# Two heads' values side by side in the array, and a new order at both ends of an expert product

## The chip, the cores and the metric

One core of a Trainium2 chip. A core has TensorE (PE: matmuls; its weight loads are listed as PEld), VectorE (DVE), ScalarE (ACT), GpSimd (POOL) and SyncE (SP, which here only issues transfers), and DMA engines that move data between HBM and the on-chip memory SBUF. Matmuls write into PSUM. Each engine works through its own queue in order; semaphores make one wait for another. The metric is the time of one execution in microseconds.

## The reference

Two layers of an encoder over 512 tokens of width 1024. A layer has a mixing block (8 retention heads and 8 dilated attention heads of 64, joined and projected), an attention over 256 memory rows, and an expert layer (128 x 128 = 16384 experts per layer, 8 heads x 16 chosen per token). The parts that matter here, shortened:

```python
for layer in range(DEPTH):
    rq, rk, rv, rg, aq, ak, av = jnp.split(rms_norm(x, norm_mix[layer]) @ w_in[layer], split_points, axis=-1)
    ret = bidirectional_retention(rq, rk * HEAD_DIM ** -0.5, rv, log_gamma)   # (q k^T * decay(i-j)) v, per head
    att = dilated_mixture_attention(aq, ak, av)      # three softmaxes over bands, mixed: one softmax with a bias
    cat = [head_rms_norm(ret) * silu(rg), head_rms_norm(att)]
    x = x + concatenate(cat) @ w_out[layer]
    x = x + memory_cross_attention(...)
    # experts: per token and head the 16 best of 128 x 128 pairs of keys
    act = gelu(einsum('thkd,td->thk', expert_down[idx], xb))
    x = x + einsum('thk,thkd->td', softmax(best) * act, expert_up[idx])
return rms_norm(x, norm_final)
```

## The kernel before

Tokens lie in 4 blocks of 128 (NB); a 512 x 512 score matrix of one head is 4 key blocks of 128 x 512. The program is written in the order of the work; a planner then puts each engine's instructions in an order of its own, by a simulated timeline, so that ready work of a later step (projections above all) fills PE where an earlier one waits. Tiles have a fixed number of buffers (bufs); a new tile of the same name waits until its buffer is free. Two number forms are used in matmuls: fp32r (one record of PE per matmul), in which an operand is split in a high and a low part by ACT and DVE (split, L112) and three products are made in place of one, and plain fp32 (two records per matmul, and two weight loads).

**The mixing block** (mix, L305) projects the values (L331), then runs two loops over the heads. heads (L279) projects queries and keys of four heads at a time and hands out one head after another.
- Retention (L336): DVE and ACT make a mask of decays (dm, two buffers), PE makes the scores of a key block (L345, keys down the partitions, queries along), DVE multiplies them by the mask (L348) into pt. Then L353, in fp32: for each query block qb and key block kb, pt's 128 x 128 part is the stationary operand and the head's 64 columns of values are streamed. The result has queries on the partitions; ACT copies it into cat (L355).
- Attention (L366): the same with a bias from HBM (L370, two buffers, 448 KB each), scores with queries on the partitions (L375), maximum on DVE (L379), exponential on ACT (L381), four transposes (L384), a copy by ACT or DVE (L387, L389), and the product with the values per query block (L391, as L353). DVE divides by the sums on the way into cat (L394). At head 7 (KH) the memory rows are normalised (mem_norm).

**The expert layer** treats blocks 0 to 2 (DB, 384 tokens) densely, with every expert, and block 3 by gathering its chosen rows (sparse, L567; POOL issues the gathers, DVE multiplies). The dense part goes by 128 rows i1 of 128 experts. For each: down (L667) loads the row's down weights, splits them, makes 24 products of 384 columns into one of two banks pj (L675) and a GELU on ACT (L678). 64 of the rows (KEPT, those with i % 8 > 3) have their down product made earlier (ahead, L681), while routes are still being computed, and stored in HBM (Cd); kept (L687) loads them again. up_parts (L698) loads the row's up weights into the pool late, splits them (w_hi, w_lo: 3 buffers), multiplies c by the gates (gt, L695) and splits c (ch, cl: 2 buffers). up (L709) makes 6 products of 512 columns per token block, accumulating over all rows in six banks of PSUM.

rest (L719) sets the order: per group of 8 rows the gates are loaded, then a full row and a kept row alternate, each with its up product at once. In between, steps of the gather loop are taken (take). The up products of the last two rows are held back and made block by block, each followed by the addition to x (L751), so that the next layer's norm, or the final one, can begin on block 0 early. layer (L593) opens and closes the pools: the pool late, whose tiles hold the up weights, lies where the routes' tiles lay before.

Of the kernel before, what the change touches and what calls it, by code (L numbers as in the profile page):

```python
# [8 lines left out]
F32 = mybir.dt.float32  # L9
F32R = mybir.dt.float32r  # L10
# [11 lines left out]
D = 1024  # L22
# [28 lines left out]
UR = 4  # L51
FIRST = (0, 1, 2, 3), (3, 0, 1, 2)
# [10 lines left out]
class Kernel:  # L63
# [77 lines left out]
    def wsplit(self, src, pool=None):  # L141

        raw = self.wload(src, pool)
        hi = (pool or self.wp).tile([128, D], F32R, name="w_hi", bufs=3)
        lo = (pool or self.wp).tile([128, D], F32R, name="w_lo", bufs=3)
        self.split(hi, lo, raw)
        return hi, lo
# [156 lines left out]

    def mix(self, l, kvp):  # L305
        nc, a, ps = self.nc, self.a, self.ps
        with ExitStack() as st:
# [28 lines left out]
            for h, q, ks in self.heads(ea, w, 0, 512, hT, 1.0, HD ** -0.5):  # L336
                dm = ea.tile([128, WREL], F32, name="dm", bufs=2)
                nc.vector.tensor_scalar(dm, relp, lg[:, h:h + 1], None, op0=OP.mult)
                nc.vector.scalar_tensor_tensor(dm, reln, lg[:, 8 + h:9 + h], dm, op0=OP.mult, op1=OP.add)
                nc.scalar.activation(dm, dm, AF.Exp)  # L340
                pts = []
                for kb in range(NB):
                    s = ps.tile([128, 512], F32, name="s", bufs=2)
                    for i in range(2):
                        nc.tensor.matmul(s, ks[i][:, kb * 128:(kb + 1) * 128], q, start=(i == 0), stop=(i == 1))  # L345
                    pt = ea.tile([128, 512], F32, name="pt", bufs=5)
                    o = 384 - 128 * kb
                    nc.vector.tensor_mul(pt, s, dm[:, o:o + 512])  # L348
                    pts.append(pt)
                po = ps.tile([128, NB, HD], F32, name="og"[h % 2])  # L350
# [15 lines left out]
            for h, q, ks in self.heads(ea, w, 2048, 2560, hT, HD ** -0.5, 1.0):  # L366
                if h == KH:
                    kT = self.mem_norm(l, sb)
                bias = ea.tile([128, WREL], F32, name="dm", bufs=2)
                nc.sync.dma_start(bias, a["att_bias"][h])  # L370
                po = ps.tile([128, NB, HD], F32, name="og"[h % 2])
                for qb in range(NB):
                    s = ps.tile([128, 512], F32, name="s", bufs=2)
                    for i in range(2):
                        nc.tensor.matmul(s, q[:, qb * 128:(qb + 1) * 128], ks[i], start=(i == 0), stop=(i == 1))  # L375
                    p = ea.tile([128, 512], F32, name="p", bufs=3)
                    m = ea.tile([128, 2], F32, name="m", bufs=4)
                    o = 384 - 128 * qb
                    nc.vector.tensor_tensor_reduce(p, s, bias[:, o:o + 512], 1.0, -3e38, OP.add, OP.max, m[:, 0:1])  # L379
                    nc.vector.tensor_scalar(m[:, 1:2], m[:, 0:1], -1.0, None, op0=OP.mult)  # L380
                    nc.scalar.activation(p, p, AF.Exp, bias=m[:, 1:2], accum_out=den[:, h, qb:qb + 1])  # L381
                    tp = ps.tile([128, 4, 128], F32, name="t", bufs=2)
                    for kb in range(NB):
                        nc.tensor.transpose(tp[:, kb, :], p[:, kb * 128:(kb + 1) * 128], self.ident)  # L384
# [554 lines left out]
```

## Time and profile before

| | us |
|---|---|
| median of 3 runs | 3547.29 (3547.2 to 3551.07) |
| the profiled execution | 3550.38 |
| its span, first to last instruction | 3548.6 |
| PE busy | 3473.6 (98%), 20844 records |
| DVE busy | 2645.4 (75%) |
| ACT busy | 1470.2 (41%) |
| mean granted PE clock | 0.991 of full speed |

The execution has these stretches in layer 0 (layer 1 repeats them about 1770 us later): retention about 53 to 158 us, attention to 292, output projection, memory attention and routes to about 850, a transition to 990 in which rows are gathered and the last kept rows made, and the dense part to 1771. A matmul's time in a row is its own, from start to a modelled end; matmuls overlap, so the pace of a run of them is the distance of starts. "Idle before" in square brackets is how long the engine stood before an instruction, and what ended it.

### The profile page before, as it was taken

The numbers are of one execution on the slowest core, as the hardware profiler recorded it, in microseconds if no ns is written. First come the engines' busy times: TensorE is split into PE (matmuls) and PEld (weight loads), VectorE is DVE, ScalarE is ACT, GpSimd is POOL, SyncE is SP. The second block draws the span as 40 slices with busy tenths as digits, with TensorE's granted clock in tenths as the row PEclk, the third lists the DMA queues.
The fourth block names the chain that finished last, engine by engine and source line by source line (L and its number), as shares of the span: only waits on it lengthen the run. The fifth ranks groups of instructions, "written<-read, shape, count | busy, mean of one in ns | idle before, by whom it ended". The sixth has DMA issues, their size and how long they took to land.

```text
span 3548.6 us, 55359 instructions
## 1 busy us (share of the span) xinstructions
PE 3473.6 (98%) x20844; PEld 3182.7 (90%) x20844; DVE 2645.4 (75%) x5722; ACT 1470.2 (41%) x2210; POOL 699.7 (20%) x518
## 2 busy tenths in 40 slices
PE   8999999999999999999999999999999999999998
PEld 7989998999888888888889899989999888888887
DVE  5565559998677788888555655599995877888885
ACT  4453544455333333333333535445553333333332
POOL 0000000002334445444100000000022443444440
PEclk9999999999999999999999999999999999999999
DMA  5252444567989999999432424446689999999992
GB/s 163 74 144 84 146 136 138 207 224 285 389 302 350 341 340 332 340 340 337 154 98 79 133 90 155 133 135 218 220 300 378 328 337 343 344 332 341 343 335 94
DMA packets 428380, 848.42 MB, mean 239 GB/s; under 512 B 28112, under 2 KB 278992, under 8 KB 421968
## 3 DMA queue, kind: packets, MB, share of 16 engines
q1 hardware_dynamic: 321360, 488.32, 41.2%
q0 software_dynamic: 73728, 268.47, 20.8%
q10 hardware_dynamic: 33024, 88.10, 6.9%
q8 instruction: 163, 2.67, 0.3%
q14 instruction: 105, 0.86, 0.1%
HBM read 754.60 MB, written 77.59 MB: 235 GB/s over the span
## 4 chain that ended last, share of the span: by engine, by line
PE 90%; DVE 6%; DMA 2%; ACT 1%; issue 1%; SPq 0%; ACTq 0%; POOL 0%; DVEq 0%; POOLq 0%
PE pj L675 28%; PE pj L174 13%; PE s L715 10%; PE t L715 10%; PE pj L190 9%; PE o L715 5%; PE g L715 5%; PE s L345 1%; DVE w_lo L114 1%; PE g L391 1%; PE s L375 1%; PE t L384 1%; PE g L353 1%; PE o L353 1%; PE g L873 1%
## 5 line engine op out<-in xcount | busy, mean ns | idle before, releaser
L114 DVE TENSOR_TENSOR w_lo<-w_raw,w_hi 128x1024 fp32r<-128x1024 f32 x696 | 849.4, 1222 | 404.1 <-ACT w_hi L113 391.7
L113 ACT ACTIVATE w_hi<-w_raw 128x1024 fp32r<-128x1024 f32 x696 | 735.3, 1060 | 981.6 <-PE g L715 342.8
L578 POOL DMA_INDIRECT row<-in_expert_down,ei x256 | 339.0, 1324 | 2308.3 <-PE g L874 916.8
L675 PE MATMUL pj<-hT_hi,w_hi 128*128 128x384 f32 x2048 | 697.7, 341 | 12.8 <-ACT c L678 10.5
L675 PE MATMUL pj<-hT_lo,w_hi 128*128 128x384 f32 x2048 | 698.8, 341 | 0.0
L675 PE MATMUL pj<-hT_hi,w_lo 128*128 128x384 f32 x2048 | 696.0, 340 | 0.8 <-DVE w_lo L114 0.6
L578 POOL DMA_INDIRECT row<-in_expert_up,ei x256 | 360.0, 1406 | 454.2 <-DVE x L590 419.3
L675 PEld LDWEIGHTS pj<-hT_hi,w_hi 128*128 128x128 f32 x2048 | 386.3, 189 | 18.3 <-ACT c L678 11.1
L675 PEld LDWEIGHTS pj<-hT_hi,w_lo 128*128 128x128 f32 x2048 | 386.1, 189 | 5.6 <-DVE w_lo L114 2.4
L675 PEld LDWEIGHTS pj<-hT_lo,w_hi 128*128 128x128 f32 x2048 | 386.2, 189 | 4.4
L590 DVE SCALAR_TENSOR_TENSOR x<-row,act,x 128x1024 f32<-128x1024 f32 x256 | 327.7, 1280 | 6.0 <-DMA row<-in_expert_up,ei 4.6
L584 DVE SCALAR_TENSOR_TENSOR row<-row,hn 128x1024 f32<-128x1024 f32 x256 | 309.4, 1219 | 19.9 <-DMA row<-in_expert_down,ei 19.5
L113 ACT ACTIVATE ch<-c 128x384 fp32r<-128x384 f32 x128 | 67.0, 523 | 280.2 <-PE g L715 240.1
L715 PE MATMUL t<-w_lo,ch 128*128 128x512 f32 x512 | 160.7, 389 | 0.0
L715 PE MATMUL t<-w_hi,ch 128*128 128x512 f32 x512 | 159.6, 389 | 0.0
L715 PE MATMUL s<-w_hi,ch 128*128 128x512 f32 x512 | 158.5, 391 | 0.0
L715 PE MATMUL s<-w_lo,ch 128*128 128x512 f32 x512 | 158.1, 390 | 0.0
L190 PE MATMUL pj<-w_hi,T_hi 128*128 128x256 f32 x640 | 156.9, 286 | 0.9 <-ACT T_hi L113 0.5
L715 PE MATMUL s<-w_hi,cl 128*128 128x512 f32 x512 | 157.8, 389 | 0.0
L715 PE MATMUL t<-w_hi,cl 128*128 128x512 f32 x512 | 157.7, 389 | 0.0
L113 ACT ACTIVATE ch<-cd 128x384 fp32r<-128x384 f32 x128 | 66.6, 520 | 208.9 <-PE g L715 208.9
L174 PE MATMUL pj<-T_hi,w_hi 128*128 128x512 f32 (+1 forms) x512 | 150.0, 341 | 2.1 <-DVE qlo L260 1.8
(260 smaller groups left out, 7291.9 us busy)
## 6 DMA issues: line engine op xcount, KB each, us to landing
w_raw<-in_down_T SPq DMA_DIRECT2D x256, 512.0 KB
w_raw<-in_expert_up SPq DMA_DIRECT2D x256, 512.0 KB
Gd<-mq ACTq DMA_DIRECT2D x48, 1024.0 KB
gt<-Gd SPq DMA_DIRECT2D x32, 1536.0 KB
w_raw<-in_peer_w_query SPq DMA_DIRECT2D x64, 512.0 KB
w_raw<-in_w_in SPq DMA_DIRECT2D x56, 512.0 KB
Cd<-c ACTq DMA_DIRECT2D x128, 192.0 KB
cd<-Cd SPq DMA_DIRECT2D x128, 192.0 KB
```

The costliest lines, as they stand in the source:

```text
L113: self.nc.scalar.activation(hi, src, AF.Copy)
L114: self.nc.vector.tensor_sub(lo, src, hi)
L174: nc.tensor.matmul(ps[:, :T], wt[k // 4][x][:, k % 4, s * 128:(s + 1) * 128], hT[y][:, k, :T], start=(k == 0 and x == y), stop=(k == KT - ...
L190: nc.tensor.matmul(ps[:, :256], hT[x][:, k, ts], wt[k // 4][y][:, k % 4, :], start=(k == 0 and x == y), stop=(k == KT - 1 and (x, y) == pa ...
L345: nc.tensor.matmul(s, ks[i][:, kb * 128:(kb + 1) * 128], q, start=(i == 0), stop=(i == 1))
L353: nc.tensor.matmul(po[:, qb, :], pts[kb][:, qb * 128:(qb + 1) * 128], rv[:, kb, h * HD:(h + 1) * HD], start=(kb == 0), stop=(kb == NB - 1))
L375: nc.tensor.matmul(s, q[:, qb * 128:(qb + 1) * 128], ks[i], start=(i == 0), stop=(i == 1))
L578: nc.gpsimd.indirect_dma_start(out=t, out_offset=None, in_=tab, in_offset=bass.IndirectOffsetOnAxis(ap=ei[:, j:j + 1], axis=0))
L584: nc.vector.scalar_tensor_tensor(t, t, 1.0, self.hn, op0=OP.mult, op1=OP.mult, accum_out=act[:, j:j + 1])
L590: nc.vector.scalar_tensor_tensor(x, t, act[:, j:j + 1], x, op0=OP.mult, op1=OP.add)
L675: k.nc.tensor.matmul(pa[:, :ND], x[:, kk, :], y[:, kk, :], start=(kk == 0 and x is dh and y is hi), stop=(kk == KT - 1 and x is dl))
L715: self.k.nc.tensor.matmul(self.acc[b, h], cc[x][:, s], uu[y][:, h * 512:(h + 1) * 512], start=(b, h) not in self.started, stop=last and x ...
```

## The change

In both head loops heads are taken in pairs. half_av makes the product with the values turned round: the head's 64 columns of values of a key block are the stationary operand, the score columns are streamed, and the result has the head's 64 dimensions on 64 partitions, the even head on 0 to 63, the odd on 64 to 127 of one bank. In the retention 512 columns are streamed per key block, in two groups of two key blocks x two heads; in the attention 128 per query block, 4 key blocks x 2 heads in a group. turned copies the bank to SBUF (ACT), transposes it back in four blocks, and a copy (retention, ACT) or the division (attention, DVE) puts both heads into cat. The masks or biases of both heads of a pair are made before the pair's scores. The memory rows' norm comes before heads 6 and 7 rather than 7.

In rest three down products (EARLY) are made before anything else, and each full row's up product is followed by the down product of a row three further on. The first up product is put behind the third down product on PE (issue_after). The last four rows (HELD) are held back for the blocks, with four buffers of w_hi, w_lo, ch and cl in place of 3, 3, 2 and 2, and five of c in place of 4; the gather loop's steps are spread over two rows fewer.

```diff
+HELD = 4
+EARLY = 3
...
-        hi = (pool or self.wp).tile([128, D], F32R, name="w_hi", bufs=3)
+        hi = (pool or self.wp).tile([128, D], F32R, name="w_hi", bufs=HELD if pool else 3)
...
+    def half_av(self, po, h, v, pt, kb):
+        r = slice(64 * (h % 2), 64 * (h % 2) + 64)
+        self.nc.tensor.matmul(po[r, :], v[:, h * HD:(h + 1) * HD], pt, start=(kb == 0), stop=(kb == NB - 1))
+
+    def turned(self, sb, po):
+        t = sb.tile([128, S], F32, name="oT")
+        self.nc.scalar.activation(t, po, AF.Copy)
+        tp = self.ps.tile([128, NB, 128], F32, name="t", bufs=2)
+        for qb in range(NB):
+            self.nc.tensor.transpose(tp[:, qb, :], t[:, qb * 128:(qb + 1) * 128], self.ident)
+        return tp
...
-                for qb in range(NB):
-                    for kb in range(NB):
-                        nc.tensor.matmul(po[:, qb, :], pts[kb][:, qb * 128:(qb + 1) * 128],
-                                         rv[:, kb, h * HD:(h + 1) * HD], start=(kb == 0), stop=(kb == NB - 1))
-                nc.scalar.activation(cat[:, :, h * HD:(h + 1) * HD], po, AF.Copy)
+            it = self.heads(ea, w, 0, 512, hT, 1.0, HD ** -0.5)
+            for m, two in enumerate(zip(it, it)):
...
+                po = ps.tile([128, 512], F32, name="og"[m % 2])
+                for k0 in range(0, NB, 2):
+                    pts = []
+                    for kb in range(k0, k0 + 2):
+                        for (h, q, ks), dm in zip(two, dms):
...
+                            pts.append((kb, h, pt))
+                    for kb, h, pt in pts:
+                        self.half_av(po, h, rv[:, kb], pt, kb)
+                tp = self.turned(ea, po)
+                nc.scalar.activation(cat[:, :, m * 128:(m + 1) * 128], tp, AF.Copy)
...
-                    for kb in range(NB):
-                        nc.tensor.matmul(po[:, qb, :], pt[:, kb, :], av[:, kb, h * HD:(h + 1) * HD],
-                                         start=(kb == 0), stop=(kb == NB - 1))
+                        for h, pt in pts:
+                            self.half_av(po[:, qb * 128:(qb + 1) * 128], h, av[:, kb], pt[:, kb, :], kb)
+                tp = self.turned(ea, po)
...
-        c = self.sb.tile([128, ND], F32, name="c", bufs=4)
+        c = self.sb.tile([128, ND], F32, name="c", bufs=5)
...
-        ch = self.late.tile([128, ND], F32R, name="ch", bufs=2)
+        ch = self.late.tile([128, ND], F32R, name="ch", bufs=HELD)
...
-            if n < NK - 2:
+            if n == 0:
+                with k.tc.issue_after(self.at):
+                    self.up(parts, 0, nb)
+            elif n < NK - HELD:
                 self.up(parts, 0, nb)
...
-            owed += left / (NK - 4)
+            owed += left / (NK - HELD - 2)
...
+        full = iter([i for i in range(NK) if i not in kept])
+        cs = [self.down(next(full)) for _ in range(EARLY)]
         for g in range(NK // GI):
             gt = self.gates(pool, g)
...
                 for i1 in pair:
-                    c = self.kept(kept[i1]) if i1 in kept else self.down(i1)
+                    c = self.kept(kept[i1]) if i1 in kept else cs.pop(0)
                     add(self.up_parts(c, gt[:, :, i1 % GI, :], i1))
+                    if i1 not in kept:
+                        cs += [self.down(i) for i in itertools.islice(full, 1)]
...
         for b in range(nb):
-            self.up(last[0], b, b + 1)
-            self.up(last[1], b, b + 1, True)
+            for i, parts in enumerate(last):
+                self.up(parts, b, b + 1, i == HELD - 1)
```

## Rows read from the trace of the kernel before

**Rows 1.** the page, busy time by engine, and the shares of the chain
```profile
PE 3473.6 (98%) x20844; PEld 3182.7 (90%) x20844; DVE 2645.4 (75%) x5722; ACT 1470.2 (41%) x2210; POOL 699.7 (20%) x518
PE 90%; DVE 6%; DMA 2%; ACT 1%; issue 1%; SPq 0%; ACTq 0%; POOL 0%; DVEq 0%; POOLq 0%
```

**Rows 2.** windows: stretch: length, busy us (instructions) per engine, PEclk, DMA share, GB/s
```profile
53.00:158.00 105.00, 104.57 (x697) 95.22 (x698) 60.20 (x86) 40.77 (x54) 0.00 (x0) 1.00 0.34 98
176.00:292.00 116.00, 112.46 (x711) 98.19 (x709) 72.62 (x193) 61.04 (x119) 0.00 (x0) 0.99 0.41 114
952.00:986.00 34.00, 26.79 (x127) 25.41 (x126) 22.23 (x31) 12.94 (x18) 8.68 (x7) 0.85 1.02 379
986.00:1754.00 768.00, 768.00 (x3713) 680.32 (x3712) 606.51 (x752) 275.67 (x373) 308.07 (x221) 1.00 0.92 321
```

**Rows 3.** timeline of PE in one retention head: start, us, engine, line
```profile
77.00 3.01 PE L353 MATMUL o<-rv,pt 128*128 128x64 f32 x26
79.82 0.48 PE L345 MATMUL s<-Q,K 128*128 128x512 f32 x1
```

**Rows 4.** lines of the retention stretch: busy, mean ns, idle before
```profile
L353 PE MATMUL o<-rv,pt 128*128 128x64 f32 x128 | 16.0, 268 | 0.0
```

**Rows 5.** timeline of PE: f32 products of 128 and of 256 columns
```profile
677.27 0.61 PE L539 MATMUL s<-keysT,b 128*128 128x128 f32 x4
677.71 0.22 PE L873 MATMUL g<-oh,oh 128*128 128x128 f16 x1
678.63 3.67 PE L174 MATMUL pj<-hq,w_raw 128*128 128x256 f32 x16
682.14 0.61 PE L539 MATMUL s<-keysT,b 128*128 128x128 f32 x4
```

**Rows 6.** timeline of PE: eight transposes and what follows
```profile
219.01 1.04 PE L384 MATMUL t<-ident,p 128*128 128x128 f32 x8
219.81 0.48 PE L375 MATMUL s<-K,Q 128*128 128x512 f32 x1
```

**Rows 7.** lines of the attention stretch
```profile
L391 PE MATMUL o<-rv,pt 128*128 128x64 f32 x128 | 15.9, 270 | 0.0
L387 ACT ACTIVATE pt<-t 128x512 f32<-128x512 f32 x16 | 9.5, 594 | 13.2 <-PE t L384 13.1
```

**Rows 8.** timeline of SP: a bias load in the attention
```profile
246.68 9.97 SPq L370 DMA_DIRECT2D dm<-in_att_bias  x2
```

**Rows 9.** timeline of PE at the start of the dense part, both layers
```profile
956.68 0.69 PE L675 MATMUL pj<-hT_hi,w_hi 128*128 128x384 f32 x1 [4.22 <-ACT c L678]
961.88 0.35 PE L675 MATMUL pj<-hT_hi,w_hi 128*128 128x384 f32 x1
2723.40 0.69 PE L675 MATMUL pj<-hT_hi,w_hi 128*128 128x384 f32 x1 [6.26 <-ACT c L678]
```

**Rows 10.** the chain in order of time: start, us, what; a run of down products
```profile
920.86 23.29 PE pj L675 x134
```

**Rows 11.** timelines of ACT and SP at the same places
```profile
935.91 7.47 SPq L138 DMA_DIRECT2D w_raw<-in_expert_up  x1
955.19 1.06 ACT L113 ACTIVATE w_hi<-w_raw 128x1024 fp32r<-128x1024 f32 x1 [8.78 <-DMA cd<-Cd]
2721.91 1.06 ACT L113 ACTIVATE w_hi<-w_raw 128x1024 fp32r<-128x1024 f32 x1 [12.72 <-DMA w_raw<-in_expert_up]
```

**Rows 12.** timeline at the change of layers
```profile
1771.52 0.34 SPq L75 DMA_DIRECT2D gain<-in_norm_mix  x1
1777.76 1.97 PE L123 MATMUL t<-ident,nr_h 128*128 128x128 f32 x8 [6.27 <-DVE nr_h L109]
```

**Rows 13.** timeline at the end
```profile
3535.90 0.39 PE L715 MATMUL o<-w_hi,cl 128*128 128x512 f32 x1
3536.13 0.39 PE L715 MATMUL g<-w_hi,cl 128*128 128x512 f32 x1
3543.57 1.28 DVE L109 SCALAR_TENSOR_TENSOR nr_h<-x,rs_y,gain 128x1024 f32<-128x1024 f32 x1
```

More of the change, by code (lines that the diff above doesn't have):

```diff
@@ L1 @@
+import itertools
 import math
@@ new lines, in mix @@
+                biases = []
+                for h, q, ks in two:
+                    bias = ea.tile([128, WREL], F32, name="dm", bufs=2)
+                    nc.sync.dma_start(bias, a["att_bias"][h])
+                    biases.append(bias)
+                po = ps.tile([128, 512], F32, name="og"[m % 2])
+                for qb in range(NB):
+                    pts = []
+                    for (h, q, ks), bias in zip(two, biases):
+                        s = ps.tile([128, 512], F32, name="s", bufs=2)
+                        for i in range(2):
+                            nc.tensor.matmul(s, q[:, qb * 128:(qb + 1) * 128], ks[i], start=(i == 0), stop=(i == 1))
+                        p = ea.tile([128, 512], F32, name="p", bufs=3)
+                        mx = ea.tile([128, 2], F32, name="m", bufs=4)
+                        o = 384 - 128 * qb
+                        nc.vector.tensor_tensor_reduce(p, s, bias[:, o:o + 512], 1.0, -3e38, OP.add, OP.max, mx[:, 0:1])
+                        nc.vector.tensor_scalar(mx[:, 1:2], mx[:, 0:1], -1.0, None, op0=OP.mult)
+                        nc.scalar.activation(p, p, AF.Exp, bias=mx[:, 1:2], accum_out=den[:, h, qb:qb + 1])
+                        tp = ps.tile([128, 4, 128], F32, name="t", bufs=2)
+                        for kb in range(NB):
+                            nc.tensor.transpose(tp[:, kb, :], p[:, kb * 128:(kb + 1) * 128], self.ident)
+                        pt = ea.tile([128, 4, 128], F32, name="pt", bufs=5)
+                        if h % 2:
+                            nc.scalar.activation(pt, tp, AF.Copy)
+                        else:
+                            nc.vector.tensor_copy(pt, tp)
+                        pts.append((h, pt))
+                    for kb in range(NB):
+                        for h, pt in pts:
+                            self.half_av(po[:, qb * 128:(qb + 1) * 128], h, av[:, kb], pt[:, kb, :], kb)
@@ L399, in mix @@
+                if m % 2:
+                    self.norm_heads(sb, cat, gcat, 2 + m // 2)
             early.close()
@@ L674, in down @@
             for x, y in ((dh, hi), (dh, lo), (dl, hi)):
-                k.nc.tensor.matmul(pa[:, :ND], x[:, kk, :], y[:, kk, :], start=(kk == 0 and x is dh and y is hi),
-                                   stop=(kk == KT - 1 and x is dl))
-        c = self.sb.tile([128, ND], F32, name="c", bufs=4)
+                self.at = k.nc.tensor.matmul(pa[:, :ND], x[:, kk, :], y[:, kk, :], stop=(kk == KT - 1 and x is dl),
+                                             start=(kk == 0 and x is dh and y is hi)).ins
+        c = self.sb.tile([128, ND], F32, name="c", bufs=5)
         k.nc.scalar.activation(c, pa[:, :ND], AF.Gelu_apprx_tanh)
```

67 lines of the change are left out of this document (24 added, 43 removed).

## The prediction

> **What bounds the kernel now.** I read the page first: TensorE (PE) is busy for 3473.6 of the 3548.6 us and the chain of waits lies on it for 90% [rows 1]. So only two things can pay: less PE time, or less of the 75 us in which PE stands still. Then the stretches: in the retention PE is busy for 104.6 of 105 us while DVE has 60 and ACT 41; in the attention 112.5 of 116, with DVE at 72.6 and ACT at 61; the dense part proper is PE without a gap (768 of 768), and its start loses 7.2 of 34 us [rows 2]. The change works in all three places.
>
> Then the price of what is replaced. The product of scores and values is 16 fp32 matmuls a head, and each is two records of PE (the groups count 512 for 16 heads x 16). One of them streams only 64 columns, yet 26 in a row take from 77.00 to 79.82, 0.1085 us each [rows 3]. An fp32 product of 128 columns takes the same, 4 from 677.27 to 677.71, 0.110 us; one of 256 takes 16 from 678.63 to 682.14, 0.219 us [rows 5]. So time goes with the columns above 128 and has a floor at about 0.108 us below, which 64 columns do not get under: with 128 stationary columns, half the time of each such product is wasted.
>
> **The change part by part.** *Values.* Removed: 8 heads x 16 x 2 = 256 records in the retention of a layer and as many in its attention, at 0.1085 us: 27.8 us each, 111 us in all four.
>
> Added in the retention: 4 matmuls a head, 64 records a layer, of 512 columns: twice the 256 column price, 0.438 us, 28.0 us if they run one after another. In the attention 256 records of 128 columns at 0.110 us: 28.2 us. So with one after another nothing is gained by the swap itself (28.0 and 28.2 against 27.8). All hangs on whether the two heads of a pair overlap: each has 64 stationary columns and writes one half of the partitions, and the loops alternate the heads. Nothing in this trace uses half the columns; the bounds are no overlap (0.438 and 0.110 us a record) and two at a time (half). I take the overlap, since a head's matmuls share neither output partitions nor stationary columns with the other's, and PE is the engine where a second, idle half is there. It is not quite half: the two records of one matmul follow each other on the same half, so a group of 8 records takes 5 steps and one of 16 takes 9. Retention: 8 groups x 5 x 0.438 = 17.5 us. Attention: 16 groups x 9 x 0.110 = 15.8 us. Gain 10.3 + 12.0 = 22.3 us a layer, **-44.6** in both.
>
> The result now comes out turned. Four transposes a pair, 16 pairs: eight stand from 219.01 to 219.81, 0.10 us each [rows 6], 64 of them: **+6.4**. Ahead of each stands a copy on ACT of 512 columns (0.594 us, as L387 [rows 7]), and in the retention a second one; they replace shorter ones. ACT (41 of 105, 61 of 116) has the room; PE fills their time with projection products, as it does now, and where no projection is left each costs its 0.6 us, 4 pairs at most, 2.4 us.
>
> Going from whole-array products to half-array ones and back happens twice a group: 24 groups a layer, 96 changes in all. The trace has no such change. From below: the transposes between other products leave no gap [rows 6], 0. From above: one small product lasts 0.268 us at a pace of 0.108 [rows 4], so 0.16 us of it is overlapped by the next, and if the array had to empty each change would lose that: 15.4 us. I take the upper end, **+15.4**, because the two records nearest to it (small fp32 products, here and in the attention with 0.270 us [rows 7]) both have this tail.
>
> The Trainium skill, page "TensorEngine Tiling (Array Packing)", under "Key Properties", says that a change of tiling mode empties the engine, while tiles of one mode run independently. By it the 15.4 us would be paid and the 44.6 us gained; no run here shows either.
>
> *Pairs.* The two heads of a pair hold both buffers of the decay mask or bias (dm), where before one was loaded ahead. In the attention the next pair's bias can only be sent for after this pair's last scores. Already now such loads wait on SP (two of them stand 9.97 us [rows 8]); SP's later entries, weight loads, wait behind them. A 512 KB load sent at 1771.52 serves a DVE step of 1.28 us that is over by 1777.76 [rows 12, 13], so it lands within 4.9 us. Of this 2.8 us are covered by the rest of the pair on PE (8 transposes 0.8, the last values 9 x 0.110, the turning 0.6 + 0.4); 2.1 us stay open where no projection is left to fill, two boundaries a layer: **+8.4**, between 0 (filled) and 4.9 x 6 boundaries = 29. In the retention the mask is made by DVE and ACT with projections beside it: 0.
>
> Values together: -44.6 + 6.4 + 15.4 + 8.4 = **-14.4**.
>
> *Three downs ahead.* At the start of the dense part of layer 0 PE stands still for 7.2 us [rows 2], 4.22 of them at one place, and in layer 1 for 6.26 [rows 9]. After the wait it runs slowly: 16 products take from 956.68 to 961.88, 0.325 us each [rows 9], where 134 in a row take 23.29 us, 0.174 each [rows 10]; the granted clock of the stretch is 0.85 in the mean [rows 2], so part of it lies at the lower of the two levels, 1.2 GHz, right behind an idle PE. These 16 lose 2.4 us, and I put the same on layer 1: 7.2 + 6.3 + 4.8 = 18.3 us in all. What ends the waits: PE waits for a GELU on ACT [rows 9], and ACT stands for 8.78 and 12.72 us behind transfers [rows 11]. SP sends for the first up row at 935.91, 20 us before PE runs again, into DMA queues that are full (share 1.02 [rows 2]). With the change three down loads and their splits stand ahead of the up rows in every queue, on SP, ACT and DVE; PE gets 3 x 24 x 0.174 = 12.5 us of products that don't need an up row. That covers a late up row; it doesn't empty the DMA queues, and the stores of kept rows still stand on ACT's queue. I take half, **-9**, between -18 and +4 (the same burst later, and one wait of 4.22 more).
>
> *Four rows held.* PE's work is the same, and there is no gap to fill in the dense part [rows 2]. What it moves is the end: products follow each other at 0.227 us (3535.90, 3536.13), so that with four rows block 0 is complete 2 x 24 x 0.227 = 10.9 us before the last product; now only the very last row goes block by block, 2.7 us. The last product ends at 3536.5, and DVE then serves three blocks in turn, the last at 3543.57 [rows 13]. With blocks 0 and 1 served before, two steps of 1.28 us go from in front of block 2's: **-2.5**; from 0 (they are late again) to -5 (their additions too). At the change of layers PE stands for 6.27 us, but for a gain row that SP sends at 1771.52, just as the last up product ends [rows 12], not for a block: 0, at best -8 (that wait and the slow clock behind it). The larger buffers (one more w_hi, w_lo and c, two more ch and cl) serve a stretch in which PE has no gap: 0, and PE itself is their cover.
>
> **Sum.** -14.4 - 9 - 2.5 = -26 on the profiled execution's own 3550.4 us (1.8 us more than its span): 3524.4. The runs' median, 3547.3, lies 3.1 us below that execution; I count from halfway, 3549, and forecast **3523**.
>
> **Rivals.** *One after another* (slower). The half-array matmuls don't overlap: 2 x (28.0 + 28.2 - 55.6) = +1.2 in place of -44.6, with turning, changes and pairs +31.4, less 11.5 at the dense part: +20, **3569**. It decides from the point where the overlap saves under 18.7 of its 44.6 us. For it: no row shows the overlap, and both halves are fed from one queue. Against it: PE starts 16 short fp16 products between 677.71 and 678.63, 0.058 us each [rows 5], so the queue is not what holds 0.438 us. 20%.
> *Cheap changes* (better). Nothing is lost between whole and half array (15.4 less), and the whole 18.3 us at the dense starts come back: -26 - 15.4 - 9.3 = -51, **3498**. For it: no gap around the transposes [rows 6]; against: full DMA queues [rows 2]. 20%.
> *The other engines take over* (no change). With less PE work the attention meets DVE's chain of score, maximum, exponential and copy, and its 12.0 us a layer shrink to 4; the dense starts give nothing because ACT still stands behind its stores: -26 + 16 + 9 = -1, **3548**. For it: DVE's 72.6 of 116 us are a mean over a stretch whose first half has projections to fill; against: PE waits there for only 3.5 us [rows 2]. 17%.
> My forecast has 43%.
>
> **How the numbers follow.** 0.2% (7 us) is about what a measurement tells from no change. Faster: 41 of the 43, the 20, and 4 of the 17: 65%. Slower: 16 of the first rival's 20 (the rest for cheap changes, which bring it to 3553) and 2 of the third's: 18%. Same: 17%. The range goes from 3493 (cheap changes and some of the 8 us between the layers) to 3567, where half of the first rival lies below.
>
> **What would show it.** Half-array records whose starts lie less than 0.438 us (retention) and 0.110 us (attention) apart, or not; gaps of 0.16 us at the changes; PE waiting for dm in the attention's second half; PE's idle time and granted clock where the dense part starts; DVE's last step some 2.5 us closer to the last product. I am wrong if the retention's stretch (105 us) shrinks by less than 3 us, or if the dense start alone moves the time.

## The result and the profile after

The changed kernel took **3596.3 us** (median; 3594.9 to 3597.1) against 3547.4 before: a ratio of 1.0134, interval 1.0122 to 1.0147. It is slower by 49 us; the forecast was 3523. The profiled execution's span went from 3548.6 to 3593.2 us, +44.6.

The page of the changed kernel, busy time, against [rows 1]:

```profile
PE 3493.7 (97%) x20524; PEld 3119.4 (87%) x20524; DVE 2647.6 (74%) x5706; ACT 1482.6 (41%) x2218; POOL 679.1 (19%) x518
```

PE has 320 records fewer, as planned, and yet 20 us more busy time. The same four stretches as in [rows 2], moved to where they lie now (length, busy us per engine, clock, DMA share):

```profile
53.00:163.00 110.00, 109.04 (x516) 72.03 (x516) 60.30 (x86) 41.61 (x53) 0.00 (x0) 1.00 0.33 92
183.00:309.00 126.00, 113.96 (x722) 86.27 (x721) 72.18 (x187) 64.10 (x123) 0.00 (x0) 0.99 0.38 110
970.00:1011.00 41.00, 29.23 (x144) 27.92 (x143) 25.00 (x34) 15.84 (x22) 7.93 (x6) 0.83 0.94 330
1011.00:1763.00 752.00, 752.00 (x3642) 667.08 (x3641) 604.36 (x750) 272.29 (x366) 294.82 (x222) 1.00 0.93 328
```

Retention grew from 105 to 110 us with PE still busy; attention from 116 to 126, and PE stands still for 12.0 of them where it stood 3.5; the start of the dense part grew from 34 to 41, with 11.8 us idle instead of 7.2. The dense part proper has no gap, as before.

Where the 44.6 us arise can be read from the starts of the first and last PE records of a stage (before, then after). The output projection of layer 0 begins at 312.3 and 328.6: **+16.3**. Its last up product starts at 1771.1 and 1792.1: +21.0, so the experts' part adds **+4.7**. Layer 1's first retention score: +20.0 (-1.0). Its output projection, 2079.3 and 2119.0: **+19.7** more. Its last up product, 3536.1 and 3583.1: **+7.3** more. The rest of the program after that is 2.4 us shorter: **-2.4**. So the head loops cost 36 us and the experts' part 10. Of the 36 us PE stands still for 18.6: its idle time from the first retention score to the output projection, in both layers, is 25.2 us where it was 6.6. The other 17.5 are PE's work, which was forecast to fall by 22.8 (values, turning and changes together).

*Why retention grew.* PE in the changed kernel, the first value products of a pair and the next ones (start, us, line, count):

```profile
101.82 0.63 PE L370 MATMUL s<-Q,K 128*128 128x512 f32 x2
102.37 1.08 PE L312 MATMUL g<-pt,rv 128*64 128x512 f32 x4
103.38 0.73 PE L370 MATMUL s<-Q,K 128*128 128x512 f32 x2
...
105.84 0.28 PE L193 MATMUL pj<-w_lo,T_hi 128*128 128x256 f32 x1
106.05 1.07 PE L312 MATMUL g<-pt,rv 128*64 128x512 f32 x2
107.05 0.73 PE L370 MATMUL s<-Q,K 128*128 128x512 f32 x2
```

Four records (one product of each head) take 1.01 us from 102.37 to 103.38, and two records (one product of one head) take 1.00 from 106.05 to 107.05. So the overlap exists and is whole: the second head costs nothing. But most products have no second head beside them. Of the 32 value products of a retention stage 22 stand alone, between scores and projections, and 10 in five groups of two: 27 groups at 1.0 us are 27 us (27.8 counted from start to start), no less than before (25.9 in the same count; the prediction had 27.8 by the pace of [rows 3]). The loops alternate the heads; the order that PE was given doesn't, because the planner sends each product as soon as its own operand is ready. In attention the same happens once a group: the first of eight goes ahead, then come seven.

```profile
217.40 0.48 PE L404 MATMUL s<-K,Q 128*128 128x512 f32 x1
217.81 0.43 PE L312 MATMUL o<-pt,rv 128*64 128x128 f32 x2
218.17 0.66 PE L413 MATMUL t<-ident,p 128*128 128x128 f32 x4
...
222.62 0.40 PE L177 MATMUL pj<-T_hi,w_hi 128*128 128x512 f32 x1
222.95 1.09 PE L312 MATMUL o<-pt,rv 128*64 128x128 f32 x14
223.97 0.55 PE L413 MATMUL t<-ident,p 128*128 128x128 f32 x3
```

14 groups of two records, 14 of fourteen and 2 of sixteen: with retention's 27 that is 57 groups a layer, 228 changes between whole and half array, not 96.

*What a change costs.* Up to 105.84 us products of 256 columns follow each other at 0.118 us; from the last of them to the value product at 106.05 it is 0.21, 0.09 too much. The two records there take 1.00 us, 0.15 more than two of the 0.423 us steps of a whole group (experiment 1). Behind them the second score product starts 0.34 us after the first, where 0.23 is usual: 0.11 more. In attention the same three parts are 0.09, 0.15 (the fourteen records take 8 steps of 0.109 us, 0.87, but 1.02 pass until the transposes) and 0.05. So a group pays about 0.35 us in retention and 0.29 in attention for in and out together, some 0.16 a change, and the 228 changes about 36 us. About half of that stands in the rows of other lines, right ahead of a group and right behind it.

*Attention's end.* What PE waited for there (205 to 330 us; total, times, longest):

```profile
PE t L126 <- DVE T_lo L465: 2.9, 1, 2.9
PE g L312 <- ACT pt L416: 2.8, 3, 2.1
PE t L320 <- ACT oT L317: 1.6, 3, 0.7
PE t L126 <- DVE cat L427: 1.3, 1, 1.3
PE s L404 <- DVE m L408: 1.1, 4, 0.5
PE t L413 <- ACT p L410: 1.0, 1, 1.0
PE t L413 <- DVE cat L427: 0.7, 2, 0.4
```

In the kernel before (199 to 312 us) it waited for:

```profile
PE t L384 <- ACT p L381: 1.9, 2, 1.6
PE t L123 <- DVE T_hi L114: 0.9, 1, 0.9
PE t L384 <- DVE T_hi L114: 0.2, 1, 0.2
```

The waits of the changed kernel are steps of softmax, of the turning, and of the norm of the memory rows (T_lo, L465). The bias (dm) can't stand in such a list, because DVE reads it and PE doesn't. DVE did wait for it, 3.8 us in layer 0 and 1.1 in layer 1, and never in the kernel before; but PE's waits for that step of DVE (m, L408) are 1.1 and 1.4 us in all, so a late bias is a small part.

*Dense start.* PE's first two waits, against [rows 9], and ACT's longest, against [rows 11]:

```profile
975.96 0.69 PE L709 MATMUL pj<-hT_hi,w_hi 128*128 128x384 f32 x1 [5.67 <-ACT c L712]
988.64 0.44 PE L709 MATMUL pj<-hT_hi,w_hi 128*128 128x384 f32 x1 [2.28 <-ACT w_hi L116]
```

```profile
974.47 1.06 ACT L116 ACTIVATE w_hi<-w_raw 128x1024 fp32r<-128x1024 f32 x1 [10.11 <-DMA w_raw<-in_expert_up]
```

A third wait of PE, 3.82 us for a w_lo at 993.08, makes up the 11.8 us. The kernel before had a wait for a down matrix too, a shorter one:

```profile
970.13 0.44 PE L675 MATMUL pj<-hT_hi,w_hi 128*128 128x384 f32 x1 [2.35 <-ACT w_hi L113]
```

And the end, against [rows 13]: the last product starts 5.0 us ahead of DVE's last step, where it was 7.4.

```profile
3583.10 0.39 PE L749 MATMUL g<-w_hi,cl 128*128 128x512 f32 x1
...
3588.11 1.28 DVE L112 SCALAR_TENSOR_TENSOR nr_h<-x,rs_y,gain 128x1024 f32<-128x1024 f32 x1
```

### The profile page after: what moved, and what is told of

Its sections match the earlier page's. It is cut to its first block, busy times and chain, and to the rows that moved or that the text cites. A ratio compares the mean times of both kernels' runs of the same rounds, so it can differ in the third digit from the quotient of the medians.

```text
span 3593.2 us, 54969 instructions
## 1 busy us (share of the span) xinstructions
PE 3493.7 (97%) x20524; PEld 3119.4 (87%) x20524; DVE 2647.6 (74%) x5706; ACT 1482.6 (41%) x2218; POOL 679.1 (19%) x518
## 5 line engine op out<-in xcount | busy, mean ns | idle before, releaser
L612 POOL DMA_INDIRECT row<-in_expert_down,ei x256 | 328.0, 1281 | 2373.7 <-PE g L915 1795.9
L612 POOL DMA_INDIRECT row<-in_expert_up,ei x256 | 350.5, 1369 | 460.4 <-DVE x L624 422.2
```

Of the source, the lines that this page charges most:

```text
L612: nc.gpsimd.indirect_dma_start(out=t, out_offset=None, in_=tab, in_offset=bass.IndirectOffsetOnAxis(ap=ei[:, j:j + 1], axis=0))
```

## The experiments

Ratios are to the kernel before, run beside each on the same chip. "Traced" is the span of one profiled execution against the 3548.6 us of the kernel before. Runs of the kernel before on one chip lie between 3544.5 and 3561.3 us, so a traced difference of a few us shows little by itself.

**1. Last head first: is it the order?**

```diff
-                    for kb, h, pt in pts:
-                        self.half_av(po, h, rv[:, kb], pt, kb)
+                    for kb, h, pt in reversed(pts):
+                        self.half_av(po, h, rv[:, kb], pt, kb ^ 1)
...
-                        for h, pt in pts:
+                        for h, pt in reversed(pts):
```

> The changed kernel, with one edit: in each group of value products the head whose weights are made last is multiplied first (the loops over the group run backwards; in retention the rows of keys of a group swap places). Work, shapes and tiles are the same. In the trace of the changed kernel 22 of the 32 value products of a retention stage stand alone, with other full-width matmuls between, and only 10 have a partner that starts 7 ns later; in attention one of eight often stands alone ahead of the other seven. Theory 'parted': the first product of a group has its operand before the others and is sent ahead alone, so the halves seldom run beside each other and each lone one pays two changes of the array's shape. With the last one first, none can go before all are there: groups of 4 and of 8 stay whole. Then retention's value products take 8 groups x (4 slots x 0.438 + about 0.15) = 15.2 us of a layer instead of 27.8, attention's 16 x (8 x 0.109 + 0.2) = 17.2 instead of 23.9, and scores some 2 to 3 us less for fewer changes: about 20 us a layer, 40 in all, near 3556 us (3548 to 3570). Rival 'starved': what was lost is TensorE waiting for softmax rows now that two heads are finished together (idle of 12.7 us between 60 and 312 us against 3.6 before); a group that waits for its last operand waits as long or longer, and the time stays at 3590 to 3605 us.

3566.0 us, ratio 1.0052 (1.0038 to 1.0066), inside the range of "parted"; traced 3563.6, 29.6 us less than the changed kernel. All groups are whole now:

```profile
101.91 1.94 PE L312 MATMUL g<-pt,rv 128*64 128x512 f32 x8
103.78 1.19 PE L370 MATMUL s<-Q,K 128*128 128x512 f32 x4
...
209.13 1.09 PE L312 MATMUL o<-pt,rv 128*64 128x128 f32 x16
210.15 1.09 PE L413 MATMUL t<-ident,p 128*128 128x128 f32 x8
```

Eight records in 1.87 us, sixteen in 1.02. Counted from each record's start to the next one's, a layer's value products take 15.8 us in retention (changed kernel 27.8, before 25.9) and 18.3 in attention (23.9 and 27.5). So "parted" holds: it made the halves useless. But PE's idle time from the first retention score to the output projection rose to 17.0 us (3.6 before, 12.7 in the changed kernel), and in layer 1 to 16.3 (3.1 before, 12.5): these 8 us more than in the changed kernel are most of the 10 by which 3556 was missed. So "starved" is a second loss beside the order; 14 of the 17 us lie between 228 and 293 us, in attention's second half.

From the first retention score to the output projection both layers together take 496.5 us (493.1 before, 529.1 in the changed kernel). PE's work there is 23.3 us less than before and its idle time 26.7 us more. So whole groups bring the head loops back to about where they were; most of the 15.0 us by which this trace is still longer than that of the kernel before lies in the experts' part.

**2 to 4. The parts alone.** Heads only (the changed kernel with the experts' part of before), experts only (with the head loops of before), and held rows only (the kernel before, with the four buffers too):

```diff
-                    c = self.kept(kept[i1]) if i1 in kept else cs.pop(0)
+                    c = self.kept(kept[i1]) if i1 in kept else self.down(i1)
```

```diff
-            it = self.heads(ea, w, 0, 512, hT, 1.0, HD ** -0.5)
-            for m, two in enumerate(zip(it, it)):
+            for h, q, ks in self.heads(ea, w, 0, 512, hT, 1.0, HD ** -0.5):
...
```

```diff
-            if n < NK - 2:
+            if n < NK - HELD:
...
-            self.up(last[0], b, b + 1)
-            self.up(last[1], b, b + 1, True)
+            for i, parts in enumerate(last):
+                self.up(parts, b, b + 1, i == HELD - 1)
```

> The head loops of the changed kernel alone; the experts' part is that of the kernel before (one down product ahead, two rows held back). Theory 'parted' (and 'starved' alike): nearly all of the loss is in the mixing stage, 17.5 us a layer by the place where the output projection's stage ends, so 3547 + 35 = 3582 us (3577 to 3589). Rival 'dense start': the three down products ahead cost most of it (TensorE idle 11.8 us at the start of the experts' part against 7.2, clock 0.83 for 40 us): then below 3570.

> The experts' part of the changed kernel alone (three down products ahead of the first up product, four up rows held back); the head loops are those of the kernel before. Theory: the start of the experts' part loses 3 to 5 us in the first layer and 5 to 8 in the second, the held rows give 2.4 back at the end: 3553 to 3560 us. Rival (my forecast's own terms, minus 9 and minus 2.5): 3536 us. Rival 'dense start' as the main loss: over 3570.

> The kernel before with one part of the change: four up rows held back for the blocks instead of two (four buffers for their operands). Theory: the gap from the last up product to the end of the program falls from 12.1 to about 9.7 us as it does in the changed kernel, and a little more may be gained where the first layer gives way to the second: 3543 to 3546 us. Rival 'no worth': the later blocks' rows make the last up products wait as long as they save: 3546 to 3550.

Heads: 3587.2, ratio 1.0109 (1.0094 to 1.0125), traced +35.1. Experts: 3558.2, ratio 1.0023 (1.0013 to 1.0033), traced +7.8. Together +42.9 of the 44.6, and 1.32% of the 1.34% by the ratios: the parts add, and each lies in the range of its first theory. Held rows: 3547.3, ratio 0.9993 (0.9984 to 1.0002), traced -3.7; by the runs no difference can be told, and 3547.3 lies in the range of "no worth". In the trace, 1.7 us of the 3.7 lie behind the start of the last up product, which is where the held rows act. PE's waits at the dense start of "experts only", and the windows:

```profile
954.51 0.69 PE L678 MATMUL pj<-hT_hi,w_hi 128*128 128x384 f32 x1 [3.75 <-ACT c L681]
970.97 0.69 PE L678 MATMUL pj<-hT_hi,w_hi 128*128 128x384 f32 x1 [5.09 <-ACT w_hi L116]
```

```profile
940.00:960.00 20.00, 16.25 (x79) 15.55 (x78) 7.11 (x10) 4.31 (x6) 2.94 (x2) 0.84 1.09 365
960.00:980.00 20.00, 13.31 (x57) 12.16 (x56) 9.25 (x12) 7.13 (x9) 2.67 (x3) 0.82 0.94 366
```

The first wait is that of before [rows 9]. The second, for the split of a down matrix that came late, was 2.35 us before; in layer 1, where PE waited for no such split before, it now waits 2.04 and 3.09 us. In both slices part of the time lies at the lower clock level (1.2 GHz), right behind the waits.

**9. Three downs only**, from "experts only":

```diff
-HELD = 4
+HELD = 2
```

> The kernel before with one part of the change: three down products ahead of the first up product (two up rows held back as before). In the experts' part alone (3558 us) TensorE stood 11.0 us between the last gate product and the first up product instead of 7.2, and at a clock of 0.83 for 40 us, waiting for w_hi and w_lo of the second and third down matrix. Theory 'weights late': all of that loss is the three downs', 4 us idle and some at the lower clock in each layer, and the held rows had given 2.6 back: 3547 + 10 = 3555 to 3561 us. Rival: the two edits harm each other (four held rows take the buffers that the early downs want), the three downs alone cost under 4 us: below 3552.

3559.5, ratio 1.0022 (1.0013 to 1.0032), traced +9.1: "weights late". PE's wait for w_hi is 5.95 us at 971.68, where it was 2.35. So the three downs cost 8 us by the ratio and 9 by the trace. That the held rows give some of it back is seen in the traces alone (+7.8 with them); the two ratios don't differ.

**5 and 6. Which stage?** Pairs with the last head first in one stage, the rest as in the kernel before. From "heads only" with experiment 1's edit, number 5 puts attention back (number 6 retention, in the same way):

```diff
-            it = self.heads(ea, w, 2048, 2560, hT, HD ** -0.5, 1.0)
-            for m, two in enumerate(zip(it, it)):
+            for h, q, ks in self.heads(ea, w, 2048, 2560, hT, HD ** -0.5, 1.0):
...
```

> Retention alone in pairs with the head made last multiplied first; attention and the experts' part as in the kernel before. Theory: in retention the pair form wins once the halves stay side by side. In the trace of the kernel with both head loops so ordered, retention's value products take 15.8 us of a layer (25.9 before), its scores 17.1 (16.2), the turning back 2.5 with its waits: 6.7 us less a layer, 13 in all, so 3534 us against 3547 (ratio 0.9955 to 0.9975). Rival 'beyond retention': TensorE does the work earlier but the stage ends with the same transfers and evacuations; ratio 0.999 to 1.001.

> Attention alone in pairs with the head made last multiplied first; retention and the experts' part as in the kernel before. Theory 'starved in attention': value products 18.3 us of a layer instead of 27.5, but TensorE idles some 13 us more between the scores of the last two pairs and the end of the stage, and changes and turning back cost the rest: 6 to 10 us more a layer, 12 to 20 in all (ratio 1.0035 to 1.006). Rival: attention gains as retention does and the loss of the ordered kernel is all in the experts' part; ratio under 1.000.

Retention: 3544.5, ratio 0.9982 (0.9973 to 0.9992), a gain, but half of what was expected, between the ranges of the theory and its rival; traced -3.6. Attention: 3569.6, ratio 1.0056 (1.0042 to 1.0071), traced +19.2, as "starved in attention" said. In number 5 the head loops themselves did gain what was expected, 14.3 us in both layers. Where the gain went can be seen in layer 0: at the output projection the lead over the kernel before is 9.3 us (303.0 against 312.3), at the last gate product (L874) 9.7, at the first up product 6.4, at the last up product 3.9. So 3.3 us went in a stretch in which the DMA queues are full (share 1.08); that they are the reason was not tested:

```profile
940.00:960.00 20.00, 14.36 (x67) 13.33 (x66) 11.07 (x15) 6.34 (x9) 4.96 (x3) 0.83 1.08 381
```

and 2.5 at the end of the dense part, where PE waited 3.25 us for the operands of a held row (ch).

**7. The memory norm a pair earlier**, from experiment 1.

```diff
-                if m == 3:
+                if m == 2:
                     kT = self.mem_norm(l, sb)
```

> The kernel with both head loops ordered last-first (3566 us), with one edit: the norm of the memory rows is put ahead of the third pair of attention instead of the fourth. In that kernel TensorE waits 1.4 + 2.9 us a layer for the rows of that norm (266.0 and 268.1 us), at a clock of 0.76 in that stretch. Theory 'norm in the way': with more work behind it the wait goes, 4 to 5 us a layer, 8 to 10 in all: 3556 to 3559. Rival 'VectorE and ScalarE bound the end of attention': TensorE waits elsewhere for the same rows and the time stays at 3562 to 3570.

3580.9, ratio 1.0084 (1.0068 to 1.0100): worse than both theories said. Idle time in layer 0 rose from 17.0 to 24.1 us: PE's two waits for the norm of the memory rows grew from 4.3 to 11.0 us. From 250 to 275 us the mean granted clock was 0.66, where experiment 1 has 0.90, so more of that stretch lies at 1.2 GHz. So the norm's place matters, in the other direction.

**8. No halves.** Experiment 1 with each value product on the whole array and a bank for each head (turned then copies each head's half out of its own bank).

```diff
-        r = slice(64 * (h % 2), 64 * (h % 2) + 64)
-        self.nc.tensor.matmul(po[r, :], v[:, h * HD:(h + 1) * HD], pt, start=(kb == 0), stop=(kb == NB - 1))
+        c = slice(h // 2 * 128, h // 2 * 128 + 128)
+        self.nc.tensor.matmul(po[h % 2], v[:, c], pt, start=(kb == 0), stop=(kb == NB - 1))
```

> The kernel with both head loops ordered last-first, but each value product takes both heads' values as its stationary operand over the full array (the other head's half of the result is not used) and has a bank of its own: no half of the array is used alone, nothing runs beside it, and the shape of the array never changes. Theory 'halves overlap': the value products go back to 64 x 0.438 = 28 us of a layer in retention and 256 x 0.109 = 28 in attention, against 15.8 and 18.3; without the 24 groups' two changes (about 0.1 each, some 5 us of a layer) that is 17 us a layer more, less what now hides idle time: 3566 + 20 to 34 = 3586 to 3600. Rival 'no overlap' (a half-width product costs as much as a full one, the gain came from fewer changes): 3556 to 3568.

3591.7, ratio 1.0119 (1.0103 to 1.0135), 26 us over experiment 1 (24 by the ratios), within the 20 to 34 of "halves overlap".

```profile
99.96 1.88 PE L312 MATMUL o<-pt,rv 128*128 128x512 f32 x4
```

Four records of one head span 1.88 us here; eight of two heads span 1.94 in experiment 1. That line is the overlap, measured. The price of the changes is gone too: from the last projection ahead of such a group to the second score product behind it 2.06 us pass, which are four steps of 0.428 and the usual 0.117 and 0.23. So that price belongs to the half-array form.

**11 to 13. What starves PE at attention's end?** Each on top of experiment 1: a fourth buffer; the gate's projection moved into attention (these lines taken from ahead of attention); the norm inside the last pair.

```diff
-                        p = ea.tile([128, 512], F32, name="p", bufs=3)
+                        p = ea.tile([128, 512], F32, name="p", bufs=4)
```

```diff
                 if m == 3:
+                    silu = N_out(1536, True)
+                    for g in range(2):
+                        self.norm_heads(sb, cat, gcat, g, silu)
+                if m == 3:
                     kT = self.mem_norm(l, sb)
```

```diff
-                if m == 3:
-                    kT = self.mem_norm(l, sb)
...
                 for qb in range(NB):
+                    if (m, qb) == (3, 2):
+                        kT = self.mem_norm(l, sb)
```

> The kernel with both head loops ordered last-first (3566 us), with one edit: four buffers instead of three for the softmax rows of attention. Theory 'buffers': with two heads in a step three buffers hold one and a half steps, VectorE waits for the transposes to free one (6.2 us in the first layer's second half of attention), and TensorE idles behind it; a fourth gives 3 to 6 us a layer back: 3554 to 3560. Rival 'chain': from a score to its weights it is one after another (bias and maximum, negation, exponential, transposes, copy), and the two heads' groups wait for its end whatever the buffers: 3562 to 3569.

> The kernel with both head loops ordered last-first (ratio 1.0052 to the kernel before), with one edit: the projection for the retention's gate (192 products of 256 columns, 23 us of TensorE a layer, which now lie between the heads of the retention) and the norm of the retention's heads are put into attention, ahead of its last pair, so that they lie between the third pair's steps. Theory 'no cover': TensorE waits in the second half of attention because nothing independent is left to run there; the idle time from the first retention score to the output projection, 17.0 us in the first layer, falls to 8 to 12, and the ratio to 1.000 to 1.003. Rival 'moved': the retention's end and the last pair lose the cover that the third pair gains; idle 15 to 20 us, ratio 1.004 to 1.007.

> The kernel with both head loops ordered last-first (ratio 1.0052), with one edit: the norm of the memory rows stands ahead of the third row block of the last pair, not ahead of the pair. That kernel waits 4.3 us a layer for those rows, with the last pair's whole softmax chain standing behind it on VectorE and ScalarE; putting it a pair earlier raised the idle time to 24 us. Theory 'norm in the way of the chain': later, the norm's steps have the pair's transposes and value products beside them: idle 17 to about 12 us, ratio 1.001 to 1.0035. Rival 'latency of the chain alone': the waits for softmax rows stay and the key projection behind the norm, which covers the last pair, starts later: idle 16 to 20, ratio 1.0045 to 1.007.

Buffers: 3557.0 (3552.2 to 3563.3), ratio 1.0013 (1.0004 to 1.0023). The runs speak for "buffers", but the trace for "chain": DVE's wait for a free `p` fell from 6.2 to 1.4 us, PE's idle time only from 17.0 to 16.6, and the span by 2.1 (the traced execution is the slowest of the ten). The size stays open. Cover: 3563.6, ratio 1.0035 (1.0022 to 1.0047), between the two forecasts; idle 17.1 us, as "moved" said. The windows of layer 0, experiment 1 first, then 12, show it moving:

```profile
230.00:258.00 28.00, 22.14 (x182) 15.03 (x180) 18.20 (x65) 16.80 (x38) 0.00 (x0) 1.00 0.43 125
258.00:293.00 35.00, 27.34 (x222) 22.21 (x221) 21.57 (x59) 16.09 (x34) 0.00 (x0) 0.90 0.15 47
```

```profile
230.00:258.00 28.00, 24.21 (x204) 20.49 (x200) 21.57 (x62) 22.31 (x37) 0.00 (x0) 0.94 0.40 146
258.00:293.00 35.00, 22.97 (x184) 19.80 (x183) 22.94 (x67) 13.97 (x29) 0.00 (x0) 0.80 0.09 31
```

The third pair stands less (3.8 us for 5.9), the last pair more (12.0 for 7.7), and there PE now waits 9.9 us for the memory norm. Norm late: 3555.6, ratio 1.0011 (1.0002 to 1.0020), traced -6.4 against experiment 1. The ratio is that of "norm in the way". PE's wait for the norm's T_lo (4.3 us in experiment 1) is down to 0.2, but idle time fell only to 15.2 us, and a wait for pt grew from 1.7 to 4.1. So the norm is a part and not the whole.

**10 and 14. What pays.** Number 10 is number 5 with number 4's edit, number 14 is number 1 with those of 4, 11 and 13 and without the early downs.

```diff
+HELD = 4
...
-            for h, q, ks in self.heads(ea, w, 0, 512, hT, 1.0, HD ** -0.5):
+            it = self.heads(ea, w, 0, 512, hT, 1.0, HD ** -0.5)
+            for m, two in enumerate(zip(it, it)):
...
+                    for kb, h, pt in reversed(pts):
+                        self.half_av(po, h, rv[:, kb], pt, kb ^ 1)
```

> A version that keeps what paid: retention in pairs with the head made last first, four up rows held back; attention and the start of the experts' part as in the kernel before. Theory: the two gains add, 6.4 (0.18%) and 2.6 (0.07%), and the wait of 3.25 us for ch at the end of the first layer's experts' part that the pair retention alone showed goes with more buffers: ratio 0.9965 to 0.998, 3536 to 3541 against 3548. Rival: what is gained early in a layer waits at the full DMA queues and nothing adds: ratio 0.998 to 0.9995.

> All that the runs so far speak for, in both stages: pairs with the last head first in retention and attention, the norm of the memory rows late, four softmax buffers, four up rows held, one down product ahead. Against the version with pairs in retention alone and four held rows (ratio 0.9949) it tells whether attention in pairs can pay once its waits are cut. Theory 'waits can be cut': value products save 9 us a layer, idle time grows by no more than that, ratio 0.993 to 0.997. Rival 'attention stays worse in pairs': two heads finished together leave too little work on TensorE, idle 14 us or more, ratio 0.9975 to 1.001.

**3533.0 us, ratio 0.9949 (0.9936 to 0.9963)** for the first: faster than both kernels, and better than the two gains added (0.9975) and than its theory expected. Why it is more is seen in part only: the 3.25 us for ch are gone, and its last up product of layer 0 leads by 10.2 us (1760.9) where retention alone led by 3.9. The second: 3540.7, ratio 0.9971 (0.9961 to 0.9980), with 13.5 us of idle time in layer 0 against 5.7; ratio and idle time lie just between its two forecasts. Its head loops take 486.0 us in both layers, less than the 493.1 before but more than the 476.5 of the first, so attention in pairs still costs (the intervals of the two ratios just touch). Attention from 230 us on with all the cures:

```profile
230.00:293.00 63.00, 53.39 (x443) 41.96 (x444) 42.01 (x129) 34.49 (x73) 0.00 (x0) 0.95 0.26 81
```

DVE is busy for 42 and ACT for 34 of 63 us: neither is full, and PE has gaps. The likeliest rest is the chain from score to weights, step after step across three engines with two heads ended together; that is read from waits, not shown by a run that shortens it. Two other things that pairs changed were not varied: the scores and the transposed weights still have two banks each (s, t), now for two heads in a step, and the copies to pt go to ACT or DVE by head, no longer by block.

## Why the prediction was wrong

- **Values, overlap (-44.6): the size would have been about right, the condition wasn't.** The step that failed is "a group of 8 records takes 5 steps and one of 16 takes 9", resting on "the loops alternate the heads". I took the loops for PE's order, and the planner's order parted the heads: value products fell by 3.1 us in both layers together (106.4 to 103.3, start to start) instead of 44.6. With the groups whole they fell by 37.6, to 68.8; without PE's idle time, which this count includes, by 42.5. They also need 4 and 8 steps, not 5 and 9.
- **Changes of the array (+15.4).** The price, 0.16 us, was right (0.15 to 0.17 measured), so "cheap changes" is out; "24 groups a layer, 96 changes in all" was wrong: there are 228, about 36 us. The Trainium skill ("TensorEngine Tiling (Array Packing)", "Key Properties") says that a change of tiling mode drains the engine and that tiles work independently. The traces agree as far as they show it: a change costs time, and the second head's records start 7 ns behind the first's.
- **Turning (+6.4).** Right for PE's work: 64 transposes at 0.109 us are 7.0. The waits for the copy ahead of them, 1.6 us a layer, come on top.
- **Pairs (+8.4, bounds 0 to 29).** The size was wrong, and most of the cause. PE's idle time in the mixing stages rose by 18.6 us, and by 26.7 with whole groups, near the upper bound; it waits for softmax rows, the turned copy and the memory norm. A bias that comes late, the cause that I gave, is there (DVE waits 4.9 us for it in both layers) but is small. My third rival had the mechanism (the other engines' chain). What I held against it, that PE waited there for only 3.5 us [rows 2], was read from a kernel in which the other head's work still covered the chain; and a chain needs no full engine.
- **These terms together.** With whole groups PE's work fell by 23.3 us, as the first three terms forecast (-22.8), in part by luck, since the steps are fewer than I counted and other lines are slower. The sum would still have failed: idle time took it back, and the three downs cost.
- **Three downs (-9): wrong sign**, +9.1 traced alone (8 by the ratio), beyond my upper end of +4. I counted their 12.5 us as products that need no up row; they need their own weights, which come through the same full DMA queues [rows 2], and PE waited 5 to 6 us for those where it had waited 2.35, and 4 to 5 in layer 1 where it had not waited.
- **Four rows held (-2.5).** The mechanism is there: the last step comes 2.4 us closer to the last product. That the whole run gains by it is not shown (ratio 0.9984 to 1.0002 alone).
- **The rival "one after another" (3569)** has the sign and 20 of the 49 us without its mechanism: the halves do overlap, they were seldom given the chance. My test for being wrong, a retention stretch less than 3 us shorter, was met: it is 5 us longer.

## What to carry to other kernels

Work that overlaps only when it is adjacent must be adjacent in the engine's own instruction order: read that order, not the loops, and multiply the operand that is made last first, so that nothing goes ahead alone. Joining two heads seems to end their softmax chains together and to take from PE the other head's work that covered them (read from the waits, not shown alone): pairs paid in retention and cost in attention, so price them where no independent work is left. Work moved ahead into a stretch with full DMA queues brings its own loads with it.

## What the runs showed of the hardware

Two products with 64 stationary columns each, on different output partitions, run wholly beside each other: their records start 7 ns apart, and four records take 1.01 us where two take 1.00. In and out of the half-array form cost 0.29 us a group in attention and 0.35 in retention, and nothing when the same products took the whole array (experiment 8). A short stand of PE costs twice: in experiment 1 it was busy for 5.71 of the 10 us around the wait for the memory norm, at a mean granted clock of 0.76, so part of what it did then ran at 1.2 GHz: the transposes right behind that wait follow each other at 0.213 us, those ahead of it at 0.109.

```profile
265.00:275.00 10.00, 5.71 (x30) 4.81 (x31) 7.34 (x17) 3.09 (x6) 0.00 (x0) 0.76 0.00 0
```
